# Other homes for the S5 layer's restacked states and Toeplitz blocks, squares as weights, and another order in the front of an S5 + SwiGLU kernel

## The chip, the core and the metric

The kernel runs on one core of a Trainium2 chip, as one launch. A core has five engines that run their own instruction streams and wait for one another by semaphores: TensorE (PE, matrix products into PSUM; its weight loads are listed as PEld), VectorE (DVE), ScalarE (ACT), GpSimd (POOL) and SyncE (SP, which issues DMA transfers here). ScalarE and GpSimd issue DMA transfers too. SBUF is the memory that the engines work from, PSUM the one that TensorE writes. The metric is the device time of one execution in microseconds.

## The reference

With these sizes the model is one layer: an S5 mixer over 1024 latent tokens of width 1024, preceded by a context of 256 tokens, and a SwiGLU network. Everything is fp32.

```
m_l = split(silu(c) @ ada_w + ada_b, 6);  m_c = split(silu(c_ctx) @ ada_w + ada_b, 6)
h_l = rms_norm(x, norm_mix) * (1 + m_l[1]) + m_l[0]          # 1024 tokens
h_c = rms_norm(ctx, norm_mix) * (1 + m_c[1]) + m_c[0]        # 256 tokens
# per direction (forward, backward), 64 groups of 16 channels, 64 complex states a group
lam_bar = exp(lam * exp(log_step));  b_bar = (lam_bar - 1) / lam * B
state[l] = lam_bar * state[l-1] + b_bar @ u[l]               # context first, latents from its last state
y[l] = Re(C @ state[l]);  y = y_fwd + y_bwd + d_skip * h_l
g = gelu(y);  y = g * sigmoid(g @ w_glu + b_glu)
x = x + m_l[2] * y
h = rms_norm(x, norm_ffn) * (1 + m_l[4]) + m_l[3]
x = x + m_l[5] * ((silu(h @ w1) * (h @ w3)) @ w2)            # hidden width 2816
out = rms_norm(x, norm_final)
```

`rms_norm` divides by the root of the mean square over the 1024 channels of a token, so the first thing to be had of x and ctx is a sum of squares for each token.

## The kernel before, in words

**Layout.** Eight neighbouring tokens form a chunk, so there are 128 latent chunks and 32 context chunks. In the S5 part a partition of the inputs is a token of a chunk and a channel of a group (8 x 16), and the chunks lie along the free dimension: X holds 64 groups of 128 latent chunks, ctxT 64 groups of 32 context chunks. States lie in RA, a region of 80.5 KB a partition, in four quarters of 20.125 KB (STQ, one for 16 groups; STE is the view of all four): 160 rows, a row for each chunk, and in it real and imaginary part, direction, and group pair. Rows 0 to 31 are context, rows 32 on latent chunks. Other regions are RC[0] to RC[3] (16 KB each), RU, RXa and RXc.

**Order.** It is written out by hand: each engine runs its instructions in the program's order. A view's overlap with another decides which instruction waits for which.

**Front (lines 160 to 670).** The squares (L175 on ScalarE, ten passes of 1024 elements) are summed over the 16 channels and over the groups by TensorE with a fixed block matrix as weights and 512 moving columns (L177). VectorE reduces the rest over the groups (L290, L291), and ScalarE takes the root (L292). VectorE meanwhile computes lam_bar's powers with `cmul` into CP and PW. `dup` (L280) brings them by identity products to the layout LB (L306, L77). `ada1` (L273) multiplies silu(c) with the first modulation weights, eight products for each of two halves; `mix_rows` (L402, L405) and `mix_cols` (L417, L418) turn the result into columns, with which `u_act`, `u_lat` and `u_ctx` scale and shift the inputs. `rs_lat` and a product on VectorE apply the reciprocal roots (L470, L471) first. `power8` (L318) and `powers` give the eighth power and its squares (LQ, SQ), which the trees and the scan use.

Then a loop over 16 blocks hb (eight sets of groups, two directions). For each block `bl_make` multiplies B and LB into two products on VectorE or GpSimd, `bl_sum` adds them by an accumulating DMA on GpSimd's queue (L378), `bl_tr` transposes them (L388 and L389 for the first four blocks, L391 for the rest) and `sums` (L509) gives each chunk's contribution to the states, copied into STQ by ScalarE (L514 to L517). Three blocks ahead of `sums` stands `bl_tr`, seven ahead `bl_make`. In the same loop `pair` and `ctx_tree` fold the context rows by pairs (on VectorE or, marked E, on GpSimd; the table CTREE says which part at which block), `ada` multiplies the rest of the modulation, `ada_load` issues its weights on SP's queue up to a given number, and `cs_load` and `cs_sign` bring the first quarter's C matrix and its signs. After the loop `ctx_tree`, `ctx_last` finish the context.

**Scan (L680 to L745).** On VectorE: 32 steps of two rows over all quarters with fills for the first quarter mixed in, then 63 steps of one row with fills for the third. Each step is four operations on STE of 128 elements a partition. Meanwhile GpSimd, TensorE and ScalarE make the C matrices (`cl_gen`, A and C steps) and the Toeplitz blocks of the first two quarters (K, T).

**After the scan.** The string that `run` reads (L860 and on) is the order: R i restacks the states of four units for one half of the chunks (`restack`, 8 copies on ScalarE, L805), P i multiplies them with the C matrices (L828) on top of the Toeplitz products within a chunk (L823), Y evicts a PSUM buffer (L879), K and T make Toeplitz blocks (`k_mats`, store kd on ScalarE's queue, load into KQ on SP's), C and F are C matrices and fills on GpSimd. Three PSUM buffers named pw serve P and the rest. `restack` writes to the homes HSe (two, in turn), `late_restack` and `late_mm` do the other half of the chunks in homes HSl, with GELU and GLU following.

**SwiGLU (from some 340 us on)** is bound by TensorE and is not touched by the diff.

Of the kernel before, what the change touches and what calls it, by code (L numbers as in the profile page):

```python
# [17 lines left out]
P = 128  # L18
# [5 lines left out]
T = 8  # L24
# [13 lines left out]
def s5_ffn_kernel(tc, a, out):  # L38
# [3 lines left out]
    with ctx:  # L42
# [70 lines left out]
        STE = view(RA, 0, [4, 161, 2, 16]).rearrange("p q c r e -> p c r q e")[:, 1:]  # L113
# [56 lines left out]
        junk = [view(RC[3], 8 + 4 * i, [2, 512]) for i in range(2)]  # L170
        psx, psc = pw([4, P]), pw([16, 32])
        for i in range(10):
            src = X[:, 8 * i:8 * i + 8] if i < 8 else ctxT[:, 32 * i - 256:32 * i - 224]
            jk, po = junk[i % 2], psx if i < 8 else psc
            S.activation(jk.rearrange("p a b -> p (a b)").rearrange("p (g c) -> p g c", c=src.shape[2]), src, AF.Square)  # L175
            for j in range(2):
                PE.matmul(po.rearrange("p g c -> p (g c)"), blk, jk[:, j], start=i % 8 == 0 and j == 0, stop=i in (7, 9) and j == 1)  # L177
        rsx, rsc = rsb[:, 0:P], rsb[:, P:P + 32]

# [110 lines left out]
        V.tensor_reduce(rsx, psx.rearrange("p g c -> p c g"), AX.X, ADD)  # L290
        V.tensor_reduce(rsc, psc.rearrange("p g c -> p c g"), AX.X, ADD)  # L291
# [174 lines left out]
        lb_psum(1, 3, 4)  # L466
        bl_make(0)
        bl_make(1)
        bl_make(2)
        V.reciprocal(rsp, rsx)  # L470
# [17 lines left out]
        for k in range(4):  # L488
            ada1(1, k)
        SY.dma_start(BXY[:, 0], a["bxy"][:, 2])  # L490
        ada_load(9)
# [68 lines left out]

        def ctx_last():
            ta, tb = (t[:, :128].rearrange("p (r q e) -> p r q e", r=2, q=4) for t in (LTb, tq))
            lq = LQ[4].rearrange("p r (q e) -> p r q e", q=4)
            dst, src = STE[:, 31], STE[:, 15]
            tt(ta, src, bc(lq[:, 0], 1, 2), MUL)
            tt(tb, src[:, ::-1], lq[:, 1:3], MUL)
            tt(dst, dst, ta, ADD)
            tt(dst, dst, tb, ADD)
# [32 lines left out]
        UACT = {0: (2, 0, 2), 1: (2, 2, 5), 2: (2, 5, 8), 3: (4, 0, 2), 4: (4, 2, 4), 5: (4, 4, 6), 6: (4, 6, 8),  # L601
                7: (6, 0, 2), 8: (6, 2, 4), 9: (6, 4, 6), 10: (6, 6, 8)}
        RSL = {1: 3, 2: 4, 4: 5, 6: 6, 8: 7}
        CTREE = {4: [(0, [0], 0, 8, E), (0, [0], 8, 16, E), (0, [1], 0, 16, E)], 6: [(0, [2, 3])],
# [5 lines left out]
        for hb in range(16):  # L610
            sums(hb)
            if hb < 2:
                for k in range(4 + 2 * hb, 6 + 2 * hb):
                    ada1(1, k)
                ada_load(12 + 4 * hb)
            if hb == 2:
                pt = mix_rows()
            if hb == 0:
# [3 lines left out]
                powers()  # L622
            if hb < 13:
# [28 lines left out]
            if hb == 7:  # L652
                ada_load(NA)
            if hb == 9:
# [21 lines left out]
        st1, st2 = (t[:, 384:512].rearrange("p (r q e) -> p r q e", r=2, q=4) for t in (LTb, ltc))  # L676
# [9 lines left out]
        KQ = [view(RA, STB * (i // 2) + 2 * (i % 2), [4, P]) for i in range(4)]  # L686
        HSe = [(RA, STB * (2 + i)) for i in range(2)]
# [38 lines left out]
        def scan():  # L726
# [6 lines left out]
            def step(lq, i, o):  # L733
                lq = lq.rearrange("p r (q e) -> p r q e", q=4)
                tt(st1, STE[:, i], bc(lq[:, 0], 1, 2), MUL)
                tt(st2, STE[:, i, ::-1], lq[:, 1:3], MUL)
# [748 lines left out]
```

## Time and profile before

| what | before |
|---|---|
| median of three runs | 1154.27 us (1153.25 to 1155.66) |
| the profiled execution's own time | 1153.81 us |
| its span | 1152.0 us |
| TensorE busy | 1008.1 us, 88% |
| weight loads | 811.0 us, 70% |
| VectorE busy | 808.6 us, 70% |
| ScalarE busy | 414.4 us, 36% |
| GpSimd busy | 638.4 us, 55% |

The profile is one execution. Its span runs from the first to the last instruction that is recorded; the time is longer by what lies around it. Busy time is the union of an engine's instructions; matmuls are pipelined, so TensorE can be listed busy without being at its peak. In the lines a name such as `ra` or `pw` is a region or tile, `x16` a number of instructions taken together, and what stands behind `<-` in brackets is what ended the wait ahead of the first of them. `EVENT_SEMAPHORE` on a queue is time that the queue's processor stood at a wait. Line numbers are those of the kernel before.

### The profile page before, as it was taken

What the parts mean: (1) busy time and instruction counts of PE and PEld (TensorE: products, weight loads), DVE (VectorE), ACT (ScalarE), POOL (GpSimd) and SP (SyncE); (2) the same over time, 40 slices, a digit from 0 to 9 for tenths busy, and PEclk for the clock granted to TensorE, in tenths of its full rate; (3) what the DMA queues carried; (4) which work ended last, traced back from release to release, by engine and by line L of the source; (5) the groups of instructions that cost most, each with busy time, mean ns of one, the idle gap of its engine ahead of it and who ended that gap; (6) DMA issues with size and microseconds to landing.
All of it is one profiled execution on the core that took longest, in us unless ns stands there. A gap on an engine that the chain in (4) does not pass through costs nothing.

```text
span 1152.0 us, 16907 instructions
## 1 busy us (share of the span) xinstructions
PE 1008.1 (88%) x6228; PEld 811.0 (70%) x6228; DVE 808.6 (70%) x1727; ACT 414.4 (36%) x870; POOL 638.4 (55%) x502
## 2 busy tenths in 40 slices
PE   7998984035696999797999999999999999999997
PEld 2575523024686998676788888888888888888875
DVE  6877899950178788798866666666666666666657
ACT  4366622045583456412322222222222222222226
POOL 0579887515537246475655555555555555555563
PEclk9998996567898999998999999999999999999999
DMA  9787676405432200110111111111111111111114
GB/s 342 263 212 165 199 251 157 88 18 124 102 124 74 81 31 17 57 55 1 55 55 55 55 55 55 56 55 56 55 55 55 55 56 55 53 47 41 45 55 146
DMA packets 54514, 103.04 MB, mean 89 GB/s; under 512 B 4384, under 2 KB 25120, under 8 KB 53408
## 3 DMA queue, kind: packets, MB, share of 16 engines
q1 hardware_dynamic: 46656, 85.57, 22.5%
q0 software_dynamic: 3456, 12.58, 5.9%
q10 hardware_dynamic: 4320, 3.81, 1.0%
q8 instruction: 49, 0.80, 0.3%
q14 instruction: 33, 0.27, 0.1%
HBM read 83.20 MB, written 6.16 MB: 78 GB/s over the span
## 4 chain that ended last, share of the span: by engine, by line
PE 65%; DVE 20%; ACT 5%; DMA 4%; POOL 3%; issue 2%; SPq 0%; ACTq 0%; POOLq 0%; DVEq 0%
PE pu L1194 10%; PE pu L1195 10%; PE pu L1193 10%; PE pd L1193 7%; PE pd L1194 7%; PE pd L1195 7%; DVE ra L70 5%; DVE ru L70 5%; DVE rxa L70 3%; DVE ltb L70 2%; PE pw L177 2%; DVE ltc L70 2%; PE pe L959 2%; PE pe L958 2%; PE pe L960 2%
## 5 line engine op out<-in xcount | busy, mean ns | idle before, releaser
L70 POOL TENSOR_TENSOR c<-rxc,c 128x512 fp32r<-128x512 f32 x128 | 169.9, 1342 | 185.2 <-ACT c L1139 181.9
L70 DVE TENSOR_TENSOR ru<-pd,ru 128x512 f32<-128x512 f32 x336 | 227.0, 690 | 2.6 <-PE pd L1195 2.5
L1195 PE MATMUL pu<-ra,c 128*128 128x512 f32 x432 | 168.4, 390 | 0.6 <-POOL c L70 0.6
L1194 PE MATMUL pu<-ra,c 128*128 128x512 f32 x432 | 168.2, 389 | 0.6 <-DVE ra L70 0.6
L1193 PE MATMUL pu<-ra,c 128*128 128x512 f32 x432 | 168.3, 390 | 0.3 <-ACT ra L1139 0.3
L1139 ACT CAST c<-rxc 128x512 fp32r<-128x512 f32 x128 | 76.7, 617 | 187.3 <-POOL rxc L70 107.4
L1193 PE MATMUL pd<-c 128*128 128x512 f32 x336 | 133.2, 397 | 10.9 <-DVE ru L70 10.9
L1194 PE MATMUL pd<-c 128*128 128x512 f32 x336 | 132.6, 395 | 0.0
L1195 PE MATMUL pd<-c 128*128 128x512 f32 x336 | 132.2, 393 | 0.0
L70 DVE TENSOR_TENSOR ru<-pu,ru 128x512 f32<-128x512 f32 x84 | 57.9, 689 | 85.9 <-PE pu L1195 51.1
L70 POOL TENSOR_TENSOR c<-ru,c 128x1024 fp32r<-128x1024 f32 x22 | 53.3, 2425 | 85.7 <-ACT c L937 77.2
L1195 PEld LDWEIGHTS pu<-ra,c 128*128 128x128 f32 x432 | 81.1, 188 | 18.6 <-POOL c L70 1.8
L1194 PEld LDWEIGHTS pu<-ra,c 128*128 128x128 f32 x432 | 81.1, 188 | 17.7 <-POOL c L70 0.9
L1193 PEld LDWEIGHTS pu<-ra,c 128*128 128x128 f32 x432 | 81.1, 188 | 17.5 <-ACT ra L1139 0.8
L70 POOL TENSOR_TENSOR c<-rxc,rxa 128x1024 f32<-128x1024 f32 x30 | 62.0, 2137 | 41.5 <-ACT rxc L576 36.5
L1193 PEld LDWEIGHTS pd<-c 128*128 128x128 f32 x336 | 64.1, 191 | 26.3 <-DVE ru L70 12.8
L1193 PE MATMUL pu<-c,c 128*128 128x512 f32 x192 | 74.9, 390 | 0.0
L1195 PE MATMUL pu<-c,c 128*128 128x512 f32 x192 | 74.8, 390 | 0.1
L1194 PE MATMUL pu<-c,c 128*128 128x512 f32 x192 | 74.7, 389 | 0.0
L1195 PEld LDWEIGHTS pd<-c 128*128 128x128 f32 x336 | 64.2, 191 | 13.5
L1194 PEld LDWEIGHTS pd<-c 128*128 128x128 f32 x336 | 64.2, 191 | 13.2
L70 DVE TENSOR_TENSOR ru<-ru,rxa 128x512 f32<-128x512 f32 (+1 forms) x62 | 61.9, 999 | 7.5 <-ACT ru L1338 3.1
(299 smaller groups left out, 2219.2 us busy)
## 6 DMA issues: line engine op xcount, KB each, us to landing
ru<-in_w SPq DMA_DIRECT2D x22, 512.0 KB, 3.5
c<-in_ada_w SPq DMA_DIRECT2D x40, 256.0 KB, 5.4
rxc<-in_w SPq DMA_DIRECT2D x38, 256.0 KB, 4.7
rxc<-in_w SPq DMA_DIRECT2D x19, 512.0 KB, 5.2
c<-c POOLq DMA_DIRECT2D x18, 512.0 KB, 6.1
ra<-in_ada_w SPq DMA_DIRECT2D x24, 256.0 KB, 5.9
ra<-in_ada_w SPq DMA_DIRECT2D x10, 512.0 KB, 11.0
ru<-in_xT SPq DMA_DIRECT2D x4, 1024.0 KB, 6.0
```

What stands on the lines that cost most here:

```text
L70: eng.tensor_tensor(out=o, in0=x, in1=y, op=op)
L177: PE.matmul(po.rearrange("p g c -> p (g c)"), blk, jk[:, j], start=i % 8 == 0 and j == 0, stop=i in (7, 9) and j == 1)
L958: PE.matmul(pz, h_[:, k], wH[:, k], start=n == 0, stop=False)
L959: PE.matmul(pz, h_[:, k], wL[:, k], start=False, stop=False)
L960: PE.matmul(pz, l_[:, k], wH[:, k], start=False, stop=n == 7)
L1139: S.copy(o[0], x)
L1193: PE.matmul(pu, wh, bh, start=start, stop=False)
L1194: PE.matmul(pu, wh, bl, start=False, stop=False)
L1195: PE.matmul(pu, wl, bh, start=False, stop=stop)
```

## The change

It has five parts.

1. **Squares as weights.** A pass of 1024 squares is now cut into eight blocks of 128 x 128, each used as weights with eight moving columns of the block matrix, into one PSUM tile of two times eight columns, a column for a token of the chunk. `row_sums` spreads these columns over 16 each with a VectorE copy, turns them with one product for the latents and four for the context, and ScalarE takes the root from PSUM. The two reductions are gone.
2. **Order in the front.** `dup` stands ahead of the first three `ada1`; `power8` and `powers` ahead of the first `bl_make`; the reciprocals and the first `rs_lat` ahead of `bl_make(1)`; the context scaling behind `bl_make(2)`; the first transposes ahead of the last row product and `mix_rows`. The second half's `ada1` come 2, 3, 3 instead of 4, 2, 2; `bl_tr(3)` moves from block 0 to 1, the second `mix_rows` from 2 to 1; `u_act` of the second set takes two portions rather than three; the portions of `ada_load` differ, and `cs_load(0)` moves from block 9 to 11.
3. **Tree.** The first quarter's first two levels (in three parts) go from GpSimd at block 4 to VectorE at blocks 4, 5 and 6.
4. **State view.** STE is indexed quarter, then real or imaginary, instead of the reverse; `products` is the common helper of `step` and `ctx_last`.
5. **Homes.** A restacked unit set has the half of the chunks as an outer index, so that each copy writes 256 contiguous elements. The first four restacks go to RC[3] (8 and 12 KB, in turn), the other four to the starts of quarters 0 and 1; the Toeplitz blocks KQ move from the starts of quarters 0 and 1 to those of 2 and 3; two of the late homes move.

```diff
-        STE = view(RA, 0, [4, 161, 2, 16]).rearrange("p q c r e -> p c r q e")[:, 1:]
+        STE = view(RA, 0, [4, 161, 2, 16]).rearrange("p q c r e -> p c q r e")[:, 1:]
...
-        psx, psc = pw([4, P]), pw([16, 32])
+        ps2 = pw([2, T])
...
-            for j in range(2):
-                PE.matmul(po.rearrange("p g c -> p (g c)"), blk, jk[:, j], start=i % 8 == 0 and j == 0, stop=i in (7, 9) and j == 1)
+            for j in range(8):
+                PE.matmul(ps2[:, i // 8], jk[:, j], blk[:, ::HC], start=i % 8 == 0 and j == 0, stop=i in (7, 9) and j == 7)
+        def row_sums():
+            me = view(RXc, 1, [2, T, HC])
+            V.tensor_copy(me, bc(ps2, 3, HC))
+            pt = pw([P + 32])
+            PE.matmul(pt[:, 0:P], me[:, 0].rearrange("p s h -> p (s h)"), ident, start=True, stop=True)
+            for b in range(4):
+                PE.matmul(pt[:, P:], me[:, 1].rearrange("p s h -> p (s h)"), ident[:, 32 * b:32 * b + 32], start=b == 0, stop=b == 3)
+            S.activation(rsb, pt, AF.Sqrt, bias=epsc[:, 0:1], scale=1.0 / D)
...
-        V.tensor_reduce(rsx, psx.rearrange("p g c -> p c g"), AX.X, ADD)
-        V.tensor_reduce(rsc, psc.rearrange("p g c -> p c g"), AX.X, ADD)
-        S.activation(rsb, rsb, AF.Sqrt, bias=epsc[:, 0:1], scale=1.0 / D)
         cmul(CP[:, 4:6], CP[:, 0:2])
         cmul(CP[:, 6:8], CP[:, 2:4])
-        for k in range(3):
-            ada1(0, k)
+        row_sums()
...
+        for k in range(3):
+            ada1(0, k)
         cmul(PW[:, 7:8], PW[:, 3:4])
...
+        power8()
+        powers()
         bl_make(0)
+        V.reciprocal(rsp, rsx)
+        V.reciprocal(rcp, rsc)
+        rs_lat(0)
         bl_make(1)
         bl_make(2)
-        V.reciprocal(rsp, rsx)
-        V.reciprocal(rcp, rsc)
-        for k in range(3, 6):
+        tt(Xc, ctxT, bc(rcp, 1, G), MUL)
+        for k in range(3, 7):
             ada1(0, k)
-        power8()
-        rs_lat(0)
-        tt(Xc, ctxT, bc(rcp, 1, G), MUL)
-        for k in range(6, 8):
-            ada1(0, k)
+        bl_tr(0)
+        ada1(0, 7)
         pt = mix_rows()
-        bl_tr(0)
         mix_cols(0, pt)
...
-        CTREE = {4: [(0, [0], 0, 8, E), (0, [0], 8, 16, E), (0, [1], 0, 16, E)], 6: [(0, [2, 3])],
+        CTREE = {4: [(0, [0], 0, 8)], 5: [(0, [0], 8, 16)], 6: [(0, [1, 2, 3])],
...
-                for k in range(4 + 2 * hb, 6 + 2 * hb):
+                for k in range(2 + 3 * hb, 5 + 3 * hb):
                     ada1(1, k)
-                ada_load(12 + 4 * hb)
-            if hb == 2:
-                pt = mix_rows()
+                ada_load(11 if hb == 0 else 16)
             if hb == 0:
                 bl_tr(2)
                 bl_make(6)
                 bl_sum(5)
-                powers()
-            if hb < 13:
+            if hb == 1:
+                bl_tr(3)
+                pt = mix_rows()
+            if 1 <= hb < 13:
                 bl_tr(hb + 3)
...
-            if hb == 7:
-                ada_load(NA)
-            if hb == 9:
+            if hb in (6, 8):
+                ada_load(NA - 4 if hb == 6 else NA)
+            if hb == 11:
                 cs_load(0)
...
-        KQ = [view(RA, STB * (i // 2) + 2 * (i % 2), [4, P]) for i in range(4)]
-        HSe = [(RA, STB * (2 + i)) for i in range(2)]
+        KQ = [view(RA, STB * (2 + i // 2) + 2 * (i % 2), [4, P]) for i in range(4)]
...
-            return view(reg, kb, [2, 2, P, 2])
+            return view(reg, kb, [2, 2, 2, 64, 2])
...
-                    dst, eng = hs[64 * ri:64 * ri + 64, gp, :, c0:c0 + nk], engs[2 * gp + ri]
+                    dst, eng = hs[64 * ri:64 * ri + 64, gp, half], engs[2 * gp + ri]
...
-        HSl = [hstate(RXc, 0), hstate(RXc, 4), hstate(RA, 2 * STB), hstate(RA, 0)]
+        HSl = [hstate(RXc, 0), hstate(RXc, 4), hstate(RA, STB), hstate(RA, 2 * STB)]
+        HSe = [hstate(*((RC[3], 8 + 4 * (i % 2)) if i < 4 else (RA, STB * (i % 2)))) for i in range(8)]
```

More of the change, by code (lines that the diff above doesn't have):

```diff
@@ L487, in s5_ffn_kernel @@
         u_ctx(1)
-        for k in range(4):
+        for k in range(2):
             ada1(1, k)
         SY.dma_start(BXY[:, 0], a["bxy"][:, 2])
-        ada_load(9)
+        ada_load(5)
         rs_lat(1)
@@ L559, in ctx_tree, with products @@
                     rot(*a_, E, ptmp)
+        def products(ta, tb, src, lq):
+            lq = lq.rearrange("p r (q e) -> p q r e", q=4)
+            tt(ta, src, bc(lq[:, :, 0], 2, 2), MUL)
+            tt(tb, src[:, :, ::-1], lq[:, :, 1:3], MUL)
         def ctx_last():
[L562 to L568, printed above, removed]
+            ta, tb = (t[:, :128].rearrange("p (q r e) -> p q r e", r=2, q=4) for t in (LTb, tq))
+            products(ta, tb, STE[:, 15], LQ[4])
+            tt(STE[:, 31], STE[:, 31], ta, ADD)
+            tt(STE[:, 31], STE[:, 31], tb, ADD)
         Cs = [view(RXc, 4, [2, 2, 16, HC]), view(RXc, 0, [2, 2, 16, HC])]
@@ L675, in s5_ffn_kernel @@
         ltc = pA.tile([P, 512], F32, tag="r4", name="ltc")
-        st1, st2 = (t[:, 384:512].rearrange("p (r q e) -> p r q e", r=2, q=4) for t in (LTb, ltc))
+        st1, st2 = (t[:, 384:512].rearrange("p (q r e) -> p q r e", r=2, q=4) for t in (LTb, ltc))
         sf = [LTa[:, 384:448], LTa[:, 448:512]]
@@ L842, in late_restack @@
             for d in range(2):
-                restack(HSl[i % 4], 4 * order[i], d, 64, 64, (S, V, S, V) if d == 0 else (S, V, E, E))
+                restack(HSl[i % 4], 4 * order[i], d, 64, (S, V, S, V) if d == 0 else (S, V, E, E))
         def run(prog):
```

27 lines of the change are left out of this document (13 added, 14 removed).

## The prediction

> **What bounds the kernel now.** I read the page first: busy shares, and the chain of work that ended last.
>
> ```profile
> PE 1008.1 (88%) x6228; PEld 811.0 (70%) x6228; DVE 808.6 (70%) x1727; ACT 414.4 (36%) x870; POOL 638.4 (55%) x502
> PE 65%; DVE 20%; ACT 5%; DMA 4%; POOL 3%; issue 2%; SPq 0%; ACTq 0%; POOLq 0%; DVEq 0%
> ```
>
> A share of 88% hides that the stages have different limits, so next came the busy times by stretch. Columns: stretch, length, then busy time and count of TensorE, its weight loads, VectorE, ScalarE and GpSimd, then granted clock, DMA share and GB/s.
>
> ```profile
> 70.00:85.00 15.00, 12.81 (x140) 9.60 (x140) 9.26 (x19) 12.89 (x38) 10.29 (x8) 1.00 0.76 182
> 85.00:108.00 23.00, 18.30 (x201) 12.65 (x194) 16.68 (x34) 17.06 (x51) 22.27 (x29) 0.95 0.60 148
> 106.00:112.70 6.70, 4.74 (x24) 2.44 (x24) 4.39 (x10) 2.02 (x6) 6.16 (x10) 0.50 0.99 199
> 185.00:247.00 62.00, 8.13 (x172) 7.21 (x172) 59.90 (x300) 3.85 (x9) 31.34 (x32) 0.50 0.36 85
> 247.00:283.00 36.00, 19.82 (x337) 17.02 (x338) 0.00 (x0) 26.41 (x62) 17.54 (x11) 0.78 0.41 86
> 420.00:1152.00 732.00, 707.15 (x3222) 586.18 (x3220) 512.69 (x751) 224.50 (x416) 410.44 (x295) 0.99 0.16 53
> ```
>
> From 420 on TensorE is 97% busy (707.15 of 732) at full clock, and no edit touches that part: what is won or lost earlier arrives there unchanged. From 85 to 108 GpSimd is the busy engine. From 185 to 247 it is VectorE with the scan, and ScalarE does 3.85 us. From 247 to 283 VectorE does nothing and ScalarE leads. So the change is priced in two places: behind the scan, and in the front, ahead of it.
>
> **Behind the scan: the copies' homes.** The time lines of VectorE's last scan step, of ScalarE, and of TensorE:
>
> ```profile
> 246.43 0.29 DVE L70 TENSOR_TENSOR ra<-ltc,ra 128x128 f32<-128x128 f32 x1
> 246.75 6.89 ACT L805 COPY ra<-ra 64x256 f32<-64x256 f32 x16 [49.76 <-DVE ra L70]
> 253.67 1.07 ACT L879 COPY ru<-pw 128x512 f32<-128x512 f32 x2
> 255.92 3.47 ACT L805 COPY ra<-ra 64x256 f32<-64x256 f32 x8
> 260.51 3.52 ACT L805 COPY ra<-ra 64x256 f32<-64x256 f32 x8
> 265.78 1.97 PE L828 MATMUL pw<-c,ra 128*64 128x128 f32 x32
> 282.72 3.76 PE L823 MATMUL pw<-ra,ru 128*128 128x128 f32 x16 [10.11 <-DMA ra<-kd]
> ```
>
> ScalarE idles 49.76 us and starts the 16 copies of R0 and R1 when the scan's last instruction ends at 246.72. Their sources (rows 31 to 94 of state quarter 0) are written by the first 32 double steps, the fills of the gaps, and the first single steps to row 95. The copies therefore do not need the last step; they wait because each destination lies in RA, where the scan also writes. It is spread over [256,2] with stride inside the address span of the scan's strided write, and the dependence is kept for the span. In the change R0 to R3 go to RC[3], where the scan writes nothing. So R0, R1 and, in the same order, their matmuls P0 and P1, two evictions and the sign pass G3 can run while the scan runs, in the 49.76 us that ScalarE has. R2 and R3 read quarter 1, between the strided write's blocks, so I let them wait for the end as before.
>
> The gain by ScalarE: 255.92 − 246.75 = 9.17 us. P3 ends at 265.78 + 1.97 = 267.75 now. Afterwards: R2 from 246.75, 3.47; two evictions, 1.07; R3, 3.52, to 254.8; then, as now from R3's end (264.03) to P3's end, 3.7 us, to 258.5. TensorE will be at half clock (0.50 up to 247, row above), and P2's and P3's second halves wait for one another's PSUM buffers (three for all): I add 2 us. P3 ends at 260.5, a gain of **7 us**, with 9.2 and 5 as bounds. The K products, their store, the Toeplitz loads (the 10.11 us wait) and P4 follow P3 by the same lengths, so 7 us pass on. GpSimd's work there (17.54 of 36 us) starts behind G3 and P2, which both come earlier. The seventh and eighth restacks at the end share homes with late ones, so one late copy now waits for P7 rather than P6; ScalarE takes it after P7 anyway: nothing, at most 1 us.
>
> **The scan** keeps its instructions and element counts. Only the order r-q-e becomes q-r-e. A step is four operations of 0.28 to 0.30 us (row at 246.43), and other access orders of the same count show no other time; I take 0, and 0.01 us an operation, 4 us over 95 steps, as the bound to either side.
>
> **The front: squares.** Grouped instructions of the first 33 us, TensorE's and VectorE's time lines:
>
> ```profile
> L177 PE MATMUL pw<-c,r 128*128 128x512 f32 x40 | 20.1, 668 | 8.3 <-ACT c L175 8.3
> L175 ACT ACTIVATE c<-ru 128x1024 f32<-128x1024 f32 x8 | 8.3, 1055 | 10.1 <-PE pw L177 7.2 <-DMA ru<-in_xT 2.9
> 28.43 0.69 DVE L291 TENSOR_REDUCE r<-pw 128x32 f32<-128x512 f32 x1 [2.74 <-PE pw L177]
> 31.47 3.67 PE L280 MATMUL pw<-ra,r 128*64 128x256 f32 x32 [0.40 <-DVE ra L70]
> 41.43 0.39 PE L389 MATMUL pw<-r,ra 128*128 128x128 f32 x2
> 41.65 0.39 PE L388 MATMUL pw<-r,c 128*128 128x128 f32 x2
> 107.96 1.94 PE L391 MATMUL pw<-r,c 128*128 128x128 f32 x8 [4.25 <-DMA c<-c]
> 115.48 1.09 PE L391 MATMUL pw<-r,c 128*128 128x128 f32 x8
> ```
>
> Removed are 20 products of 512 columns (40 passes, 20.1 us from 8.28 to 28.39). Added are 80 with 128x128 weights and 8 columns. The nearest price is a product with 128x128 weights and 128 columns: two passes, one every 41.65 − 41.43 = 0.22 us. 80 × 0.22 = 17.6 us; eight columns stream less, but each still loads its weights twice. At half clock four such products take 1.94 us instead of 1.09, 0.48 each. With some 5 us cold at the start the squares end at about 28.5, as now. Bounds: ScalarE's ten passes of 1.055 end near 21 (7 us earlier); all cold, 8.3 + 80 × 0.48 = 46.7 (18 later).
>
> The Trainium skill ("TensorE: Matmul & The Clock Gate", section "LDWEIGHTS (loading the stationary operand)") gives the load's time as the columns divided by 1.2 in ns, 107 ns for 128, which speaks against small moving sides. By it 160 loads would be an estimated 17.1 us; the row's 0.22 for two passes agrees.
>
> VectorE loses two reductions of 0.69 us and no longer stalls on them ahead of the last power products, so the duplication (31.47 now) waits only for the squares, one short copy and five small products: about 29.5, **2 us earlier** (bounds 0 and 3). The 12 row products that stood ahead of it follow.
>
> **The front: powers first.** VectorE's and GpSimd's time lines:
>
> ```profile
> 34.30 2.02 POOL L70 TENSOR_TENSOR c<-c,c 128x1024 f32<-128x1024 f32 x1 [33.85 <-DVE c L77]
> 40.24 2.02 POOL L70 TENSOR_TENSOR ra<-c,c 128x1024 f32<-128x1024 f32 x1
> 57.15 4.53 DVE L70 TENSOR_TENSOR rxa<-rxc 128x64 f32<-128x64 f32 x1
> 57.29 4.30 POOL L70 TENSOR_TENSOR c<-c,c 128x1024 f32<-128x1024 f32 x2
> 65.10 0.21 DVE L70 TENSOR_TENSOR r<-rxc 128x64 f32<-128x64 f32 x1
> 36.65 1.21 DVE L70 TENSOR_TENSOR c<-c,lbt 128x1024 f32<-128x1024 f32 x1
> 38.91 0.95 DVE L470 RECIPROCAL ltb<-r 128x128 f32<-128x128 f32 x1
> 41.43 2.28 DVE L70 TENSOR_TENSOR ru<-ra,ltb 128x2048 f32<-128x2048 f32 x1
> 44.85 0.43 PE L417 MATMUL ltb<-ra,r 128*128 128x64 f32 x2
> 52.60 2.39 PE L509 MATMUL pw<-ru,c 128*64 128x160 f32 x32
> ```
>
> An operation that takes 0.21 us at 65.10 took 4.53 at 57.15, beside two GpSimd operations of 4.30 together. Operations with a PSUM operand (36.65, 1.21 us beside the GpSimd passes from 34.30 to 42.26) are not stretched. The powers now come right behind the eighth power, at about 37, while GpSimd's four passes run, moved 2 us forward, to 40.3. So VectorE stands until about 40.3, finishes the powers 3.6 us later (as from 61.7 to 65.3 now), at 44, and only then does the reciprocals (0.95 and, a quarter as long, 0.35), the lattice scaling and two passes of 1.21 each, and the context scaling, 2.28: 7.2, so 51. The mixing columns need that, and stand at 44.85 now; TensorE reaches them with row products and transposes at about 45, and idles some 5 us. First chunk sums at about 57 instead of 52.60 (**+4.5**; 1 if VectorE is not held, 7 if the next GpSimd work holds it too), and the third sums, behind the respread row products and transposes, as late. VectorE in turn is free of the 8.2 us from 57.15 to 65.31. Between 70 and 85 TensorE has 2.2 us idle and VectorE 5.7, so I let **2 us** of it be absorbed (0 to 4).
>
> The Trainium skill ("SBUF — State Buffer", section "SBUF: two separate sides") has the two engines share one port pair under an exclusive lock held for a whole instruction, with VectorE's two-SBUF-input operations taking part. The 4.53 agrees; without it the term would be +1, not +4.5.
>
> **The front: the tree.** GpSimd's time line, then VectorE's:
>
> ```profile
> 90.03 1.42 POOL L70 TENSOR_TENSOR rxc<-ra,r 128x256 f32<-128x256 f32 x2
> ...
> 98.76 1.74 POOL L378 DMA_DIRECT2D c<-c  x2
> 107.85 1.22 DVE L70 TENSOR_TENSOR c<-c,lbt 128x1024 f32<-128x1024 f32 x1 [5.53 <-DMA c<-c]
> 108.99 0.42 DVE L70 TENSOR_TENSOR ltb<-ra,lta 128x256 f32<-128x256 f32 x1
> ```
>
> Twelve GpSimd operations (90.03 to 98.8, 8.7 us) go, so the DMA issue queued behind them comes 8.7 us sooner. TensorE's 4.25 us wait at 107.96 goes, and the half clock behind it: 4.74 us busy at 0.50 from 106 to 112.7 would be 2.4 at full clock. That is **−6.65** (bounds 0 and −9: the loads of SP's queue, now fewer at a time, may still delay the landing). VectorE gets 12 operations of 0.42, started every 0.34 to 0.45: 4.4 us, covered by its 6.3 us idle between 85 and 108. Without that cover the last chunk is 4.4 late. The last chunk's tail on VectorE, up to the scan, keeps its instructions.
>
> The dup's 2 us is inside the 4.5. Front: +4.5 − 2 − 6.65 = **−4** (−10 to +3).
>
> **Other moves.** The modulation loads on SP's queue come in other portions (5 and 11 for 9 and 12; up to the twentieth at iteration 6 and the twenty-fourth at 8, instead of all at 7), row products 2, 3, 3 for 4, 2, 2, the second mixing rows and one transpose group an iteration elsewhere, two activation portions for three: the same instructions, 0 in sum, 1 us as the bound. The load of the C matrices moves from iteration 9 to 11, two past on SP's queue:
>
> ```profile
> L573 SPq EVENT_SEMAPHORE  x1: 13734/13734/13734, 99.9 to 99.9; - x1
> L573 SPq DMA_DIRECT2D rxc<-in_cxy x1: 562/562/562, 113.6 to 113.6; - x1
> L576 ACT ACTIVATE rxc<-rxc,r x4: 722/722/734, 128.9 to 254.8; 128x512 f32<-128x512 f32 x4
> ```
>
> SP's queue stands 13.7 us in front of this load now, with modulation loads queued behind it, and issues it at 113.6. The sign pass that needs it runs from 128.9, 15 us later. Issued an iteration (some 4 us) later, and landing within the 9.06 us that the slow transfer above took (98.8 to 107.85), it is there by 127: nothing. If it lands later, ScalarE's sign pass holds the copies out of PSUM queued behind it, for which TensorE waits: at most 2 us, inside the front's bounds.
>
> **Sum.** The profiled execution took 1153.81 (span 1152.0 and 1.8 around it), 0.46 under the median 1154.27. 1153.81 − 4 − 7 = **1143**.
>
> **Rivals.**
> A. The late first sums are not absorbed and the landing stays late: front 0, 1147. For: VectorE, busy 16.68 of 23 us from 85 to 108, gets 4.4 more. Against: GpSimd's 8.7 us stood right ahead of the DMA.
> B. Slower: TensorE stays at half clock through the squares, because 8-column passes are short. Place: 8 to 47 us; price 18 at the duplication, which feeds everything in the front. 1143 + 17.5 = 1160. It decides once the squares end later than 28.4 + 11 = 39.4. For: the clock was 0.50 in the scan's stretch with 8.13 us of TensorE work in 62. Against: 128x128 loads back to back at 41 kept 0.22.
> C. The copies still wait (another buffer's reader or the source too): 1150.
> D. R2 and R3 also start under the scan: P0 to P3 are done, K begins at 247 instead of 267.7, and with the front 1143 − 13 = 1130.
> E. VectorE is not held by GpSimd, or recovers fully: front −10, 1137.
>
> **How the numbers follow.** My forecast 0.43 (1138 to 1148), A 0.16, B 0.10, C 0.13, D 0.08, E 0.10. About 0.2%, 2.3 us, is what a measurement of this kernel can tell from no change. C at 1150 is within reach of "same" by its own front bound, two fifths of its chance; all of B is slower. Faster 0.85, same 0.05, slower 0.10. D below 1133 and B above 1154 are left out, so the range is 1133 to 1154.
>
> **What would show it.** Right: ScalarE's first L805 copies near 200 us; P3 about 13.5 us behind the scan's end; the squares' last pass at 28 to 29; a powers operation of some 3 us on VectorE near 37; first sums near 57; no wait of TensorE for the DMA near 100; scan start near 143. Wrong: copies starting at the scan's end (C), a granted clock of 0.5 over the squares (B), or a scan start at or behind 147 (A).

## The result, and the profile after

The changed kernel takes 1142.86 us (median of four runs, 1142.15 to 1143.35) against 1154.38 us before (1153.25 to 1155.66): a ratio of 0.9899, with a 95% interval of 0.9882 to 0.9917. The forecast was 1143, in a range of 1133 to 1154. The number is right to 0.2 us, and most of the working behind it is wrong: the front, forecast 4 us shorter, became 27 us longer, and the part behind the scan, forecast 7 us shorter, became 38 us shorter. Two rivals that had a chance of 0.10 and 0.08 came true together, with opposite signs.

The page of the changed kernel, busy times and shares:

```profile
PE 1030.9 (90%) x6358; PEld 844.7 (74%) x6358; DVE 809.6 (71%) x1738; ACT 414.8 (36%) x870; POOL 629.8 (55%) x490
```

TensorE is busy 22.8 us more in a span that is 10.5 us shorter (1141.5). The shares do not say where; the time lines do. First VectorE's scan, its first operation in the kernel before, and the first and the last one in the changed kernel:

```profile
146.87 0.29 DVE L70 TENSOR_TENSOR ltb<-ra,lta 128x128 f32<-128x128 f32 x1
```

```profile
174.09 0.29 DVE L70 TENSOR_TENSOR ltb<-ra,lta 128x128 f32<-128x128 f32 x1
...
273.66 0.29 DVE L70 TENSOR_TENSOR ra<-ltc,ra 128x128 f32<-128x128 f32 x1
```

The scan lasts as long as before (174.09 to 273.95 after, 146.87 to 246.72 before, 99.9 us each), so the new state view costs nothing in it, but it starts **27.2 us later**. From its end to the end of the span there are 1141.5 − 273.95 = 867.55 us, where there were 1152.0 − 246.72 = 905.28: **37.7 us less**. 27.2 − 37.7 = −10.5, the difference of the spans.

**The front.** TensorE's time line of the changed kernel, from the squares to the first chunk sums (L177 squares, L290 dup, L283 row products, L425 mixing columns, L517 chunk sums):

```profile
8.35 34.30 PE L177 MATMUL pw<-r,c 128*128 128x8 f32 x160 [8.35 <-ACT c L175]
...
45.44 6.17 PE L290 MATMUL pw<-ra,r 128*64 128x256 f32 x32
51.55 2.74 PE L283 MATMUL prow<-c,r 128*2 128x512 f32 x12
...
68.22 0.69 PE L425 MATMUL ltb<-ra,r 128*128 128x64 f32 x2 [3.94 <-DVE ra L70]
...
77.20 2.39 PE L517 MATMUL pw<-ru,c 128*64 128x160 f32 x32
```

The 160 passes of the squares take 34.30 us, one every 0.214 us, and end at 42.65 instead of 28.39. The dup behind them takes 6.17 us where the same 32 matmuls took 3.67 before; only the row products at 51.55 have their old 2.74 again. So TensorE ran at half pace up to some 50 us; the trace's own records of the clock, in the last section, say the same. The mixing columns come 23.4 us late (68.22 against 44.85), the first sums 24.6 (77.20 against 52.60).

**Behind the scan.** ScalarE's time line of the changed kernel (L813 are the restacks):

```profile
224.65 7.02 ACT L813 COPY c<-ra 64x256 f32<-64x256 f32 x16 [0.98 <-DVE ra L70]
...
233.94 3.50 ACT L813 COPY c<-ra 64x256 f32<-64x256 f32 x8
...
238.56 3.52 ACT L813 COPY c<-ra 64x256 f32<-64x256 f32 x8
...
257.87 3.39 ACT L813 COPY ra<-ra 64x256 f32<-64x256 f32 x8 [0.40 <-DVE ltc L70]
273.98 3.34 ACT L813 COPY ra<-ra 64x256 f32<-64x256 f32 x8 [12.72 <-DVE ra L70]
```

R0 and R1, R2, R3 and R4 all run while the scan is still going. Of R0 to R5 only R5 waits for its end, 12.72 us. TensorE, which idled under the scan before, does P0 to P3 there; its P4 starts at 268.59, behind the Toeplitz loads, 5 us ahead of the scan's end.

### The profile page after: what moved, and what is told of

Same layout as the page of the kernel before. It is cut to its first block, busy times and chain, and to the rows that moved or that the text cites. A ratio compares the mean times of both kernels' runs of the same rounds, so it can differ in the third digit from the quotient of the medians.

```text
span 1141.5 us, 17167 instructions
## 1 busy us (share of the span) xinstructions
PE 1030.9 (90%) x6358; PEld 844.7 (74%) x6358; DVE 809.6 (71%) x1738; ACT 414.8 (36%) x870; POOL 629.8 (55%) x490
## 3 DMA queue, kind: packets, MB, share of 16 engines
q1 hardware_dynamic: 46656, 85.57, 22.8%
## 4 chain that ended last, share of the span: by engine, by line
PE 64%; DVE 21%; ACT 4%; issue 2%; DMA 1%; POOL 1%; ACTq 0%; DVEq 0%; POOLq 0%; SPq 0%
PE pu L1203 10%; PE pu L1204 10%; PE pu L1202 10%; PE pd L1202 7%; PE pd L1203 7%; PE pd L1204 7%; DVE ra L70 6%; DVE ru L70 5%; DVE rxa L70 3%; DVE ltb L70 2%; PE pw L517 2%; DVE ltc L70 2%; PE pe L968 2%; PE pe L967 2%; PE pe L969 2%
## 5 line engine op out<-in xcount | busy, mean ns | idle before, releaser
L1202 PE MATMUL pd<-c 128*128 128x512 f32 x336 | 133.3, 397 | 10.9 <-DVE ru L70 10.9
L70 DVE TENSOR_TENSOR ru<-pu,ru 128x512 f32<-128x512 f32 x84 | 57.9, 689 | 85.4 <-PE pu L1204 50.6
```

The lines of the kernel that those rows point to most:

```text
L70: eng.tensor_tensor(out=o, in0=x, in1=y, op=op)
L1202: PE.matmul(pu, wh, bh, start=start, stop=False)
```

## The experiments

Each kernel below is compared with the kernel before on the same chip. Two experiments can stand on different chips, on which the kernel before took 1151.4 to 1154.4 us, so a difference of 2 or 3 us between their medians alone tells little. Parts are numbered as in the change: 1 squares, 2 order, 3 tree, 4 state view, 5 homes.

### The homes alone

The kernel before with parts 4 and 5, as the diff above has them, and nothing else.

> The kernel before with only the state view and the homes changed (parts 4 and 5). Theory 1 (all of R0 to R4 run under the scan and only R5 waits for its end, whatever the front does): scan ends at 246.7 as before, behind it all is as in the changed kernel (1141.5 - 273.95 = 867.5 us to the end), so 246.7 + 867.5 + 1.8 = 1116. Theory 2 (the forecast: only R0 and R1 move): 1147. Rival (R0 to R3 move but K products, stores and GpSimd then bind): about 1130.

Measured: 1115.65 us, ratio 0.9670 (0.9655 to 0.9684). That is theory 1 to half a microsecond, and 27 us faster than the whole change. ScalarE's time line:

```profile
196.71 7.03 ACT L805 COPY c<-ra 64x256 f32<-64x256 f32 x16 [0.99 <-DVE lta L70]
...
231.05 3.38 ACT L805 COPY ra<-ra 64x256 f32<-64x256 f32 x8 [0.40 <-DVE ltc L70]
247.26 3.35 ACT L805 COPY ra<-ra 64x256 f32<-64x256 f32 x8 [12.83 <-DVE ra L70]
```

The copies start 50 us ahead of the scan's end, as in the changed kernel. The scan's own start is 0.5 us from the kernel before. All of the 38 us is won by parts 4 and 5.

### The state view, and the layout of a home

Which of the two, and what in part 5? First part 5 without part 4:

```diff
-        STE = view(RA, 0, [4, 161, 2, 16]).rearrange("p q c r e -> p c q r e")[:, 1:]
+        STE = view(RA, 0, [4, 161, 2, 16]).rearrange("p q c r e -> p c r q e")[:, 1:]
```

(with the old `step` and `ctx_last` beside it).

> As the run with the homes alone (1115.65), but with the old state view (part 5 without part 4: order r-q-e and the old scan step). Theory 1 (the view's order decides whether copies of quarter 1 are held to the scan's end): R0 and R1 run under the scan, R2 and R3 wait for its end at 246.7, as my forecast said for both views; time 1144 to 1148. Theory 2 (only the destinations count): R0 to R4 under the scan as with the new view, 1115 to 1117.

Measured: 1115.61 us, ratio 0.9674 (0.9659 to 0.9688): theory 2. Part 4 does nothing for the time, and my forecast's reason for holding back R2 and R3, that their source in quarter 1 lies between the blocks of the scan's write, is wrong under either view. Then the region without the contiguous layout:

```diff
-        HSe = [(RA, STB * (2 + i)) for i in range(2)]
+        HSe = [(RC[3], 8 + 4 * (i % 2)) if i < 4 else (RA, STB * (2 + i % 2)) for i in range(8)]
```

> The kernel before with the new state view and only one thing of part 5: R0 to R3 go to RC[3], in the old spread layout (256 pairs with stride); R4 to R7, the late homes and the Toeplitz homes stay as before. Theory 1 (for R0 to R3 the region counts, not the contiguous layout): R0 to R3 run under the scan, R4 and R5, whose homes still lie spread in RA, wait for its end; P4 waits for R4, 3.4 us more than with all homes: 1118 to 1120. Rival (the contiguous layout is needed for it): the copies start at 246.7, 1150 to 1154.

Measured: 1118.11 us, ratio 0.9697 (0.9678 to 0.9716): theory 1. ScalarE's time line:

```profile
196.58 7.05 ACT L805 COPY c<-ra 64x256 f32<-64x256 f32 x16 [0.99 <-DVE ra L70]
205.90 3.50 ACT L805 COPY c<-ra 64x256 f32<-64x256 f32 x8
210.52 3.52 ACT L805 COPY c<-ra 64x256 f32<-64x256 f32 x8
245.86 6.75 ACT L805 COPY ra<-ra 64x256 f32<-64x256 f32 x16 [16.83 <-DVE ra L70]
```

R0 to R3, homed outside RA, run under the scan in the old strided layout too (each copy writes two runs of 128 elements there, not the 256 pairs of the expectation). R4 and R5, still homed at the starts of quarters 2 and 3, wait for the scan's end. One line of the diff brings 35 of the 38 us.

### Where a home in RA may lie

In the run with the homes alone R4 (home at 0 of RA) does not wait and R5 (home at 20.125 KB, the start of quarter 1) does. A step that writes row 96 or later of all four quarters reaches from 12 KB of RA to its end. Moved: the homes of R5 and R7.

```diff
-        HSe = [hstate(*((RC[3], 8 + 4 * (i % 2)) if i < 4 else (RA, STB * (i % 2)))) for i in range(8)]
+        HSe = [hstate(*((RC[3], 8 + 4 * (i % 2)) if i < 4 else (RA, 4 * (i % 2)))) for i in range(8)]
```

> The run with the homes alone (1115.65), with R5's and R7's home at 4 KB of RA instead of the start of quarter 1 (20.125 KB). Theory 1 (a copy is held to the scan's end when its home lies between the first and the last byte that a scan step writes, from row 96 of quarter 0, at 12 KB, to quarter 3): 4 KB lies ahead of it as R4's 0 does, R5 starts right behind R4 at about 235, P5 no longer waits, 3.5 to 5 us less: 1110.5 to 1112.5. Rival (R5's source, the second four units of quarter 2, holds it): R5 at 247 as before, 1115 to 1116.5.

Measured: 1112.07 us, ratio 0.9648 (0.9628 to 0.9668). ScalarE's time line:

```profile
230.41 6.77 ACT L805 COPY ra<-ra 64x256 f32<-64x256 f32 x16 [0.40 <-DVE ra L70]
```

R4 and R5 now run back to back under the scan: theory 1, by the trace. (The time alone would not show it: 3.6 us by the medians, 2.5 by the ratios, whose intervals overlap.) Homes at 0 and 4 KB are not held; homes at 20.125 (the homes alone), 40.25 and 60.375 KB (the run above and the kernel before) are, though the scan writes none of those rows while they wait. For the homes of these ScalarE copies the rule of theory 1 fits all five places. The wait is one that the program puts.

It is not a rule for every write into RA, and why it holds for these copies stays open. GpSimd's fills of quarter 1 in the kernel before, and the Toeplitz loads of the run with the homes alone, also write between the first and the last byte of a scan step, and are not held to the scan's end (246.72 and 247.22). The first writing row of the fills, and P4, which needs the loads into the starts of quarters 2 and 3:

```profile
187.50 1.52 POOL L70 TENSOR_TENSOR ra<-ra,c 128x256 f32<-128x256 f32 x2
```

```profile
241.22 4.08 PE L823 MATMUL pw<-ra,ru 128*128 128x128 f32 x16 [11.78 <-DMA ra<-kd]
```

P4 starts 6 us ahead of the scan's end; the four loads for P4 and P5 were issued from 233.3 to 237.7. So whether a home is held has to be read from a trace, buffer by buffer.

### The squares

Put back: the fixed block matrix as weights with 512 columns, and the two reductions, in the changed kernel.

```diff
-            for j in range(8):
-                PE.matmul(ps2[:, i // 8], jk[:, j], blk[:, ::HC], start=i % 8 == 0 and j == 0, stop=i in (7, 9) and j == 7)
+            for j in range(2):
+                PE.matmul(po.rearrange("p g c -> p (g c)"), blk, jk[:, j], start=i % 8 == 0 and j == 0, stop=i in (7, 9) and j == 1)
...
-        row_sums()
+        V.tensor_reduce(rsx, psx.rearrange("p g c -> p c g"), AX.X, ADD)
+        V.tensor_reduce(rsc, psc.rearrange("p g c -> p c g"), AX.X, ADD)
+        S.activation(rsb, rsb, AF.Sqrt, bias=epsc[:, 0:1], scale=1.0 / D)
```

> The changed kernel with the old squares (fixed block matrix as weights, 512 moving columns) and the two reductions, put where row_sums stood; all else as changed. Theory 1 (the squares as weights ran at half clock and hold the whole front back, and the scan's end sets the rest): squares end at 28.4 instead of 42.7, dup takes 3.7 instead of 6.2 us, first chunk sums near 57 instead of 77.2, time 20 us below the changed kernel, about 1123. Rival (VectorE with the tree is the bound of the front, so the front only recovers in part): first sums earlier but scan start no more than 10 us earlier, about 1133.

Measured: 1122.56 us, ratio 0.9728 (0.9714 to 0.9743): theory 1, 20.3 us below the changed kernel. TensorE's time line:

```profile
8.33 19.76 PE L177 MATMUL pw<-c,r 128*128 128x512 f32 x40 [8.33 <-ACT c L175]
28.02 3.82 PE L280 MATMUL pw<-ra,r 128*64 128x256 f32 x32
```

The first sums stand at 57.13 in this run, 20.1 us earlier than in the changed kernel. The other way round, the new squares alone on the kernel before (the first two hunks of the diff on squares and sums):

> The kernel before with only the squares as weights and row_sums (part 1). Theory 1: squares end 14.3 us later and dup runs at half clock, 2.5 more: the scan starts some 17 us later, 1171. Rival (the later stages of the front absorb it): at most 8 us, below 1162.

Measured: 1171.97 us, ratio 1.0153 (1.0136 to 1.0170). The price is 18.2 us there. Dup starts 17.9 us later than in the kernel before (49.38 against 31.47): 14.2 because the squares end late (42.63), 2.8 for `row_sums` (VectorE's copy and five products, up to 45.42) and 1.3 because the 12 row products ahead of dup still run slowly (4.03 us instead of 2.74), less the 0.4 us that TensorE waited ahead of dup before.

What keeps them slow, the weight loads or the short moving side? The changed kernel again, with all 128 columns of the block matrix moving:

```diff
-        ps2 = pw([2, T])
+        ps2 = pw([2, P])
...
-                PE.matmul(ps2[:, i // 8], jk[:, j], blk[:, ::HC], start=i % 8 == 0 and j == 0, stop=i in (7, 9) and j == 7)
+                PE.matmul(ps2[:, i // 8], jk[:, j], blk, start=i % 8 == 0 and j == 0, stop=i in (7, 9) and j == 7)
...
-            V.tensor_copy(me, bc(ps2, 3, HC))
+            V.tensor_copy(me.rearrange("p a s h -> p a (s h)"), ps2)
```

> The changed kernel with the squares as weights as changed but with all 128 columns of the block matrix moving instead of eight (each sum comes out 16 times, so row_sums copies instead of broadcasting); same result. Theory 1 (the clock stays at half because short moving sides count for little): with 128 columns the clock rises after some 5 us, 80 products at 0.22 end near 28, time 15 to 20 us below the changed kernel. Rival (two 128x128 weight loads a product are slow at any clock or keep the clock down by themselves): squares end at 42 to 47, time 1143 to 1147.

Measured: 1122.99 us, ratio 0.9733 (0.9718 to 0.9747): theory 1. The groups of instructions of the first 60 us, in the changed kernel and then here (matmuls, then their weight loads; behind the bar busy time and the mean of one in ns):

```profile
L177 PE MATMUL pw<-r,c 128*128 128x8 f32 x160 | 34.3, 361 | 8.3 <-ACT c L175 8.3
L177 PEld LDWEIGHTS pw<-r,c 128*128 128x128 f32 x160 | 34.2, 333 | 8.3 <-ACT c L175 8.3
```

```profile
L177 PE MATMUL pw<-r,c 128*128 128x128 f32 x160 | 20.5, 296 | 8.3 <-ACT c L175 8.3
L177 PEld LDWEIGHTS pw<-r,c 128*128 128x128 f32 x160 | 20.3, 212 | 8.3 <-ACT c L175 8.3
```

The same 160 loads, with sixteen times the columns streamed between them, take 20.5 us instead of 34.3. The passes come every 0.213 us at first in both runs. With 128 columns they come every 0.112 from 13.3 us on; with eight they stay at 0.213 to the end, and the pace doubles only within dup, at 50.6. More work for TensorE is faster here, because it lets the clock rise: the trace's records of the clock begin at those times (last section). The edit also made the moving columns adjacent, where the eight stood 16 elements apart; whether their number or their spacing counts was not separated.

### The order in the front

The run with the homes alone, plus part 2 with the old squares and the tree on GpSimd.

> The run with the homes alone (1115.65), plus the new order in the front (part 2), with the old squares and the tree on GpSimd. The changed kernel with old squares was 1122.56, so order and tree together cost 6.9. Theory 1 (the order costs: powers, reciprocals and scaling ahead of the mixing columns, 3.6 us there, kept to the scan): 1119 to 1122. Rival (the order costs nothing, the tree all): 1115 to 1116.

Measured: 1122.15 us, ratio 0.9726 (0.9705 to 0.9747): theory 1 in sign, 6.5 us dearer than the homes alone, just above its upper end. TensorE's time line:

```profile
48.50 0.69 PE L417 MATMUL ltb<-ra,r 128*128 128x64 f32 x2 [3.97 <-DVE ra L70]
...
57.13 2.39 PE L509 MATMUL pw<-ru,c 128*64 128x160 f32 x32
...
75.89 0.66 PE L405 MATMUL pw<-r,ra 128*128 128x128 f32 x4 [1.16 <-ACT ra L402]
```

TensorE idles 3.97 us ahead of the mixing columns, for VectorE, which does the powers first; and the second mixing rows wait too. First sums at 57.13, 3.8 us behind the homes alone (53.33). Then only what is ahead of the loop:

```diff
+        power8()
+        powers()
         bl_make(0)
+        V.reciprocal(rsp, rsx)
+        V.reciprocal(rcp, rsc)
+        rs_lat(0)
         bl_make(1)
```

(and dup ahead of the first row products, and the rest of the first two hunks on order; the two reductions stay ahead of the last power products.)

> The run with the homes alone (1115.65), plus the part of the new order ahead of the loop only (dup first, powers first, transposes ahead of the mixing rows); the loop's order, its loads and portions as before. All of the order cost 6.5. Theory 1 (the idle TensorE time ahead of the mixing columns, 3.97 us, is carried to the scan): 1119 to 1120. Theory 2 (the whole 6.5 comes from ahead of the loop): 1121.5 to 1122.5. Rival (it is absorbed, and the loop's moves cost): 1115 to 1117.

Measured: 1125.07 us, ratio 0.9765 (0.9746 to 0.9783), 9.4 us dearer, above both theories. TensorE's time line shows a second price:

```profile
30.48 3.67 PE L280 MATMUL pw<-ra,r 128*64 128x256 f32 x32 [3.08 <-DVE ra L70]
...
50.93 0.69 PE L417 MATMUL ltb<-ra,r 128*128 128x64 f32 x2 [4.11 <-DVE ra L70]
```

Dup waits 3.08 us for the power products, which stand behind the reductions. Before, twelve row products of 2.74 us filled that time; with dup first they no longer do. So this run mixes two causes. Dup starts 2.4 us later than with the whole order (30.48 against 28.04); if that passes on in full, an estimate of 7 us is left for the pieces ahead of the loop, about all of the 6.5. It is an estimate and not shown, and how much the moves within the loop cost or bring by themselves stays open.

### The tree

The run with the homes alone, plus part 3.

```diff
-        CTREE = {4: [(0, [0], 0, 8, E), (0, [0], 8, 16, E), (0, [1], 0, 16, E)], 6: [(0, [2, 3])],
+        CTREE = {4: [(0, [0], 0, 8)], 5: [(0, [0], 8, 16)], 6: [(0, [1, 2, 3])],
```

> The run with the homes alone (1115.65), plus the tree on VectorE (part 3). Theory 1 (the forecast's term): the DMA issue comes 8.7 us sooner, TensorE's wait and half clock near 100 to 112 go, scan start up to 6.6 us earlier, 1109 to 1112. Rival (VectorE becomes the bound of blocks 4 to 6): scan start 3 to 5 us later, 1118 to 1121.

Measured: 1116.53 us, ratio 0.9677 (0.9658 to 0.9697): neither. It is the time of the homes alone within what the two intervals can tell. The wait for the DMA is gone and another has its place. TensorE with the homes alone, then TensorE and ScalarE with the tree on VectorE:

```profile
109.06 1.91 PE L391 MATMUL pw<-r,c 128*128 128x128 f32 x8 [4.62 <-DMA c<-c]
123.48 0.76 PE L509 MATMUL pw<-ru,c 128*64 128x160 f32 x8 [0.29 <-ACT ra L517]
```

```profile
106.80 2.40 PE L509 MATMUL pw<-ru,c 128*64 128x160 f32 x16 [4.85 <-ACT rxa L341]
123.49 0.77 PE L509 MATMUL pw<-ru,c 128*64 128x160 f32 x8 [0.29 <-ACT ra L517]
```

```profile
105.21 0.27 ACT L373 COPY lbt<-c 128x128 f32<-128x128 f32 x1 [4.48 <-DVE ra L70]
```

VectorE's tree, now longer at block 6, ends at 105.17. ScalarE's copy L373 writes the first half of the PSUM tile lbt, in whose other half the tree keeps a temporary, and waits 4.48 us for the tree; behind the copy stand the copies out of PSUM for which TensorE waits, 4.85 us, with half clock behind it (16 matmuls in 2.40). By 123.48 the two runs stand at the same instruction at the same time.

If so, the tree's upper levels belong at a block with no tree. Tried on the run with R5's home at 4 KB:

```diff
-        CTREE = {4: [(0, [0], 0, 8, E), (0, [0], 8, 16, E), (0, [1], 0, 16, E)], 6: [(0, [2, 3])],
+        CTREE = {4: [(0, [0], 0, 8)], 5: [(0, [0], 8, 16)], 10: [(0, [1, 2, 3])],
```

> As the run with R5's home at 4 KB, plus the first level of the tree on VectorE at blocks 4 and 5, and its other levels at block 10, which has none now, instead of block 6. Theory 1 (the tree's gain was eaten because ScalarE's copy L373 waited 4.48 us for the tree at block 6, and TensorE behind it): with that wait mostly gone too, the scan starts 3 to 5 us earlier, 3 to 5 us below the other run, 1106 to 1109. Rival (VectorE's 4.4 us of added work must be paid wherever it stands): no gain, within 1.5 us of the other run.

Measured: 1111.40 us, ratio 0.9648 (0.9617 to 0.9678), the same ratio as without it. The front does as theory 1 says and the total as the rival says. ScalarE's wait is 1.47 us in place of 4.48, and the scan's second operation starts at 144.58 instead of 147.30, 2.7 us earlier. But the end did not follow: P4 starts 1.95 us earlier, P6 0.2, and the first GELU 0.6 (276.28 against 276.87). TensorE's P4 and P6 with R5's home at 4 KB alone, then P4, part of P5 and P6 with the tree at block 10:

```profile
240.71 3.84 PE L823 MATMUL pw<-ra,ru 128*128 128x128 f32 x16 [11.16 <-DMA ra<-kd]
...
262.68 4.02 PE L823 MATMUL pw<-ra,ru 128*128 128x128 f32 x16 [7.21 <-DMA ra<-kd]
```

```profile
238.76 4.18 PE L823 MATMUL pw<-ra,ru 128*128 128x128 f32 x16 [11.62 <-DMA ra<-kd]
...
247.26 1.13 PE L823 MATMUL pw<-ra,ru 128*128 128x128 f32 x8 [0.27 <-DMA ra<-kd]
...
262.50 3.62 PE L823 MATMUL pw<-ra,ru 128*128 128x128 f32 x16 [7.80 <-DMA ra<-kd]
```

With six restacks (R0 to R5) under the scan, its end (246.94 and 244.22) is no longer what P4 to P6 wait for: P4 and P6 wait for the loads of the Toeplitz blocks, which follow their stores. Why the loads gain less than the scan was not looked into.

### Dup first, without the early powers

On the last run, the piece of part 2 that the forecast counted as a gain:

```diff
-        V.tensor_reduce(rsx, psx.rearrange("p g c -> p c g"), AX.X, ADD)
-        V.tensor_reduce(rsc, psc.rearrange("p g c -> p c g"), AX.X, ADD)
-        S.activation(rsb, rsb, AF.Sqrt, bias=epsc[:, 0:1], scale=1.0 / D)
         cmul(CP[:, 4:6], CP[:, 0:2])
         cmul(CP[:, 6:8], CP[:, 2:4])
-        for k in range(3):
-            ada1(0, k)
+        V.tensor_reduce(rsx, psx.rearrange("p g c -> p c g"), AX.X, ADD)
+        V.tensor_reduce(rsc, psc.rearrange("p g c -> p c g"), AX.X, ADD)
+        S.activation(rsb, rsb, AF.Sqrt, bias=epsc[:, 0:1], scale=1.0 / D)
...
+        for k in range(3):
+            ada1(0, k)
         cmul(PW[:, 7:8], PW[:, 3:4])
```

> The run with R5's home at 4 KB and the tree at blocks 4, 5 and 10 (1111.4), plus the one piece of the new order that my forecast counted as a gain: the reductions behind the power products and dup ahead of the first three row products; powers and all else as before. Theory 1 (of the new order only the early powers cost; dup first gains): dup starts at about 28 instead of 31.1, first chunk sums and scan start about 3 us earlier; behind the scan the Toeplitz loads eat part of it as they did with the tree, so 1108 to 1110. Rival (the mixing columns wait for other work on VectorE or TensorE): scan start within 1 us, 1110.5 to 1112.

Measured: 1109.58 us, ratio 0.9621 (0.9600 to 0.9642). Dup starts at 28.10 instead of 31.14, but the first sums only 0.5 us earlier (51.78 against 52.26) and the scan no earlier (144.99 against 144.58 for its second operation): the rival, in the trace. TensorE works from 28 us to the first sums in both runs with only one wait of 0.69 us, beside the 0.40 us ahead of dup that goes here; so dup first changes the order of its work and hardly its end. The medians differ by 1.8 us, on different chips, and the intervals overlap, so no gain over the run before can be told. It is the fastest median of all, 33 us below the changed kernel's.

## Why the prediction was right, and where it was wrong

The total is right by coincidence. Against its steps:

- **Squares** (forecast: end at 28.5, "as now"; bound 46.7). The step that failed is the choice of 0.22 us for a product at full clock, taken from products with 128 columns. Measured: 0.43 us for a product of two passes, end at 42.65, and a price of 20.3 us in the changed kernel (18.2 on the kernel before). Rival B, with 18 us and a chance of 0.10, is what happened, for the reason it gave: with 128 columns instead of eight the same kernel is 19.9 us faster. The row behind "against" in B showed 128x128 loads that kept 0.22, but it also showed 128 columns streaming with them.
- **The load time.** By the Trainium skill ("TensorE: Matmul & The Clock Gate", section "LDWEIGHTS (loading the stationary operand)") the 160 loads were an estimated 17.1 us; the trace has 34.3, twice as much. The Trainium skill (the same title, section "What's actually happening") says that the clock is throttled by default and that activity releases it, after at least one busy window of about 3.4 us. Here 34 us of weight loads one behind another, with eight columns each, did not release it.
- **Dup 2 us earlier.** True only with the old squares (28.02 instead of 31.47); and where dup came 3.0 us earlier by itself, the first sums gained 0.5, since TensorE has the same work ahead of them.
- **Powers first** (+4.5 at the first sums). With the old squares the sums stood at 57.13 against 52.60: the size is right. The reason is only half right. The changed kernel's two passes of GpSimd and VectorE's operations beside them:

```profile
54.54 2.02 POOL L70 TENSOR_TENSOR c<-c,c 128x1024 f32<-128x1024 f32 x1
56.52 2.02 POOL L70 TENSOR_TENSOR ra<-c,c 128x1024 f32<-128x1024 f32 x1
```

```profile
55.98 0.66 DVE L70 TENSOR_TENSOR rxa<-rxc 128x64 f32<-128x64 f32 x1
...
57.54 1.41 DVE L70 TENSOR_TENSOR rxc<-rxc 128x64 f32<-128x64 f32 x2
```

  VectorE's two-SBUF-input operations end just behind the end of the GpSimd pass beside them (56.64 behind 56.56, 58.95 behind 58.54). That fits their being held, but for some 0.5 and 1.0 us: the first got in between two passes, where the forecast had VectorE stand up to the end of the last. Why the one in the kernel before took 4.53, beside two passes, stays open. The rest of the delay is plainly VectorE's order: 4.5 us of powers and 7.2 us of other work ahead of the mixing columns.
- **2 us absorbed.** Wrong. With the order alone the scan starts 5.6 us later (153.21 against 147.58 for its second operation); the 3.8 us at the first sums grew.
- **Tree −6.65.** Wrong: 0. The wait for the DMA went, as forecast, and a wait of ScalarE for VectorE took its place, 4.85 us on TensorE. I had looked for cover in VectorE's idle time and not for what is queued behind it on ScalarE.
- **Scan 0.** Right: 99.9 us before and after.
- **Behind the scan −7.** Wrong, by the step that lets R2 and R3 wait for the scan's end because of their source. They do not: 37.7 us, of which R0 to R3's region gives all but some 3. That the copies waited because of their destination was right, and so was the way out of RA; that any destination within the span waits was too wide, as the fills and loads show. This is rival D, chance 0.08; D's 13 us for it was too small too, since it let the rest follow the scan's end by the old lengths, while K products, stores, loads, R4 and P4 also moved under it.

So −38.1 (homes), +20.3 (squares), +6.5 (order) and +0.4 (tree, the changed kernel with old squares against the order alone, 1122.56 − 1122.15) add to −10.9, and the change measured −11.5. Of the other rivals, A came half true: the late first sums were not absorbed, but the landing was no longer what TensorE waited for. C did not happen. E did not either: the front lost, although VectorE was hardly held. Nothing in the trace of before said that R2's source holds it: R2 ran at 255.92 there, in its turn on ScalarE and without a wait of its own. That step, the costliest to the working, rested on no row.

## What to carry to other kernels

When a wait names the last of many writes, ask whether the waiting instruction needs that write at all, and try its buffer elsewhere: moving the first four restacks to a region that the scan does not write was worth 35 us here, while the squares, the order and the tree together cost 27. Making TensorE's work smaller by making its moving side short can cost more than it saves; price it by a row with the same number of columns, or by the half clock. And an edit of many parts whose total comes out as forecast proves none of the parts until each has been run alone.

## What was not expected of the hardware

The clock stayed low through 34 us in which TensorE was listed busy without a break. The stretch of the changed kernel's squares, columns as in the prediction:

```profile
8.00:42.00 34.00, 33.65 (x158) 33.65 (x158) 14.59 (x84) 10.98 (x11) 0.00 (x0) 1.00 1.03 380
```

Its granted clock reads 1.00, while the passes come every 0.213 us (against 0.112 for the faster ones with 128 columns) and the dup behind them takes 6.17 us instead of 3.67. The column misleads here: it is worked out from records in the trace that have a start and a clock, and counts what lies ahead of the first record as full clock. The first record, full clock, starts at 50.54 us in the changed kernel, where the pace doubles within dup. It starts at 13.27 with 128 columns and at 13.71 in the kernel before, where the passes with 512 columns go from one every 0.85 us to one every 0.43. So the clock was released about 5 us after TensorE's start in those two, and in the changed kernel only about 5 us after the dup's start, at 45.44. The dup has 256 moving columns.
